# Two key pages turned within the query list, and two more loaded behind them

## The chip, the cores and the metric

The kernel runs on one core of a Trainium2 chip. The metric is the device time in microseconds (us) of one execution. TensorE (PE) multiplies, VectorE (DVE), ScalarE (ACT) and GpSimd (POOL) do elementwise work, and SyncE (SP) does no arithmetic and issues most of the DMAs.

## What is computed

One inference step of a two-layer decoder trunk: layer 0 mixes tokens with a conformer convolution, layer 1 with stick-breaking attention, and a gated ConvFFN follows each. There are 512 tokens of a new prompt and 8 sequences of 4 new tokens each, which also attend to 256 cached tokens, held in 2 pages of 128 tokens per sequence. The part that matters here is the attention:

```python
qkv = (h @ attn_w_qkv[a]).reshape(b, t, 3, N_HEADS, HEAD_DIM)
k_past = jnp.take(cache_k[a], page_table, axis=0)...      # 8 sequences x 2 pages
z = einsum('bqhd,bkhd->bhqk', q, k_all) * HEAD_DIM**-0.5 + bias
log_fail = where(valid, log_sigmoid(-z), 0)
after = cumsum(log_fail, axis=3, reverse=True) - log_fail
weights = where(valid, exp(log_sigmoid(z) + after), 0)
out = einsum('bhqk,bkhd->bqhd', weights, v_all)
```

## The kernel before, in words

Activations lie in memory with the model dimension on the partitions: `xT` is 128 x 8 x 544, for 512 prompt and 32 new tokens. A float32 matrix product is made of three matmuls on a high and a low part: ACT casts the weights to a high part `whi` (L398), DVE subtracts it to get the low part `wlo` (L401), and PE runs whi·XH, whi·XL, wlo·XH. The raw weights come in 1 MB loads (`raw54` and so on) into two buffers. The load for a buffer is issued on SP at L361, within the function of the last `wlo` that reads the buffer, so it stands in SP's order where the planner put that subtraction.

A planner (`Plan`) sets the order of the work. Each operation is listed with an engine, a cost in us and what it reads and writes. `run` then plays the list with these costs and emits each engine's instructions in the order in which the play starts them. At run time the engines keep that order, and semaphores keep the dependencies. A page load is planned as 2 us on SP and 6 us to land. SP is taken as busy for 0.7 us with any operation.

Two of these lists meet here.

- The first one ends with `queries` (from L1775): the rest of the first ConvFFN, the norm, and the queries `qT`. The last four chunks of the queries use a Strassen-like product (`query_quad`), whose inputs are made with three temporaries of 544 columns in the unused end of `kT` (`inputs`, L1489 and L1537; ring `tt2`). ACT and DVE bring the products from PSUM into `qT` (L1883, L1886). The list ends on SP: `xT` is saved to DRAM, so that its memory can hold pages, and pages 0, 1 and 2 are loaded into `page_t[0..2]` (columns 0 to 3071 of `xT`) by `key_page` (L2041 to L2045). A page is 4 DMAs of 128 KB.
- The second one is the attention. `keys` and `values` project chunk after chunk (`project`, 24 matmuls for each half: 256 columns, then 288). Below, k0, k1, v0, k2 are the first projections, with the weights 148, 149, 150 and 151, and A and B are their halves. `keys` evacuates `kT` on ACT (L2201), transposes the new rows on DVE (`kr`, L2207) and stores them with 4 DMAs (L2212). `pair` makes units of attention between prompt tokens: logits `z` on PE (L2432), exp, ln and exp on ACT, a clamp (L2451), a scan (L2462) and a product (L2467) on DVE, then the transposition `t` on PE (L2474) and the products `av`.

The cached keys are used in `page_logits(m)`, for m from 0 to 3, four pages each. DVE transposes two pages into `kt`, which is the unused end of `kT`, and two into buffers of the ring `e` (all at L2283). Then PE makes 32 logit matmuls into `dz` (L2301): 16 from `kt`, then 16 from the `e` buffers. Page i goes into `page_t[i % 3]`, once DVE has transposed page i-3. All 16 key pages pass this way, and after them the 16 value pages, which POOL gathers (L2050).

PE is in order, as are all engines here: if an instruction waits, all behind it on that engine wait too.

Of the kernel before, what the change touches and what calls it, by code (L numbers as in the profile page):

```python
# [18 lines left out]
D = 1024  # L19
# [5 lines left out]
T = SEQ + NS  # L25
# [39 lines left out]
LATE_X = 0.6  # L65
LIFT = 10
PAGE_BUFS = 3
LATER = 1
WAITS = (2,5)
DUE = (3,1)  # L70
# [180 lines left out]
def tile_trunk(  # L251
# [9 lines left out]
    dve, act, pool, pe = nc.vector, nc.scalar, nc.gpsimd, nc.tensor  # L261
# [84 lines left out]
    class Ring:  # L346
# [28 lines left out]
        def prep(self, later=None, halves=False):  # L375
# [35 lines left out]
            else:  # L411
                later.insert(min(LATER, len(later)), low)

# [308 lines left out]
    plan = Plan(E_CONV, 0.12, CONV_SHIFTS)  # L722
# [14 lines left out]
    def psum(tag):  # L737
        def make():
            if tag == "acc":
                taken.append(tag)  # L740
            return bank(tag, uid(tag))

        return plan.tile(tag, banks[tag], make)
# [363 lines left out]
    for c in range(0, NC, 2):  # L1107
# [9 lines left out]
        for cc in range(2):  # L1117
            plan.op("act", 0.33, lambda c=c, cc=cc, pt=pt: act.copy(
                ext_s[:, c + cc, :, 0:PAST], pt()[:, cc * 240:(cc + 1) * 240].rearrange("p (b t) -> p b t", b=NB)),
                r=[pt, "junk"], w=[("past", c + cc)])  # L1120
# [124 lines left out]
    for h, (c0, n) in enumerate(STREAMS):  # L1245
        if h:
            layer_norm(1)
        for g in (0, 4):
            for i in range(4):
                c = g + i  # L1250
# [5 lines left out]
        if not h:  # L1256
# [8 lines left out]
            r=[nrm.acc[0]], w=[ms])  # L1265
    plan.op("act", 0.34, lambda: act.activation(rs()[:, :n], ms()[:, :n], AF.Sqrt, bias=eps_t[:, 0:1], scale=1.0),
            r=[ms, "table"], w=[rs])
    plan.op("dve", 1.7, lambda: dve.reciprocal(rs()[:, :n], rs()[:, :n]), w=[rs])
    for c in range(NC):
# [3 lines left out]
                r=[rs, ("x", c, 0)], w=[u])  # L1273
# [4 lines left out]
            r=[u, ("XH", c, 0)], w=[("XL", c, 0)], lift=NLIFT)  # L1278
# [26 lines left out]
    def ffn(l, before, after):  # L1305
# [10 lines left out]
        plan = Plan(E_FFN)  # L1316
# [459 lines left out]
        def queries(s):  # L1776
# [35 lines left out]
            for h, st in enumerate((SA, SB)):  # L1812
                c0, n = st
                for c in range(NC):
# [3 lines left out]
                            r=[pt], w=[("x", c, h)])  # L1818
# [32 lines left out]
            for i in range(ready, len(plan.ops)):  # L1851
                e, cost, f, deps = plan.ops[i]
# [45 lines left out]
            plan.op("dve", 0.6, decode_columns, r=["numbers"], w=["tables"])  # L1898
            plan.op("dve", 0.9, decode_masks, r=["tables"])
            for j in range(PAGE_BUFS):  # L1900
                plan.op("sp", 2.0, lambda j=j: key_page(page_t[j], j), r=["saved", "numbers"])
            return s

        first = slot_no[0]
# [21 lines left out]
        if l == 0:  # L1926
            s = queries(s)
# [10 lines left out]
        after = after()  # L1938
# [93 lines left out]
    att = {}  # L2032
    xsave = scratch.tile([P, NC * T], F32, name="xsave")
    xflat = xT.rearrange("p c t -> p (c t)")
    page_t = [xflat[:, i * D:(i + 1) * D] for i in range(PAGE_BUFS)]
    numbers = []
# [4 lines left out]
    def key_page(t, j):  # L2041

        pages = cache_k[0, bass.ds(numbers[j], 1)].rearrange("o (q p) (x h) d -> o x p q (h d)", p=32, x=4)
        for x in range(4):
            nc.sync.dma_start(out=t[32 * x:32 * x + 32, :].rearrange("p (q r) -> p q r", q=4), in_=pages[0, x])  # L2045
# [3 lines left out]
    def gather(t, j, src):  # L2049
        pool.indirect_dma_start(out=t, out_offset=None, in_=src,  # L2050
                                in_offset=bass.IndirectOffsetOnAxis(ap=idx[:, j:j + 1], axis=0))

    ffn(0, nrm, None)
    qT, kT, kT_s, dz = (att[k] for k in ("qT", "kT", "kT_s", "dz"))
# [19 lines left out]
    def place_q(bg):  # L2074
        for rows, x, q, src in placed(bg):
            dst = Qz[rows].rearrange("p (c q) (b r) -> p q c b r", q=4, b=4)[:, q, :, :, 4 * x:4 * x + 4]
            pool.tensor_copy(dst, src)
# [33 lines left out]
    plan = Plan()  # L2111
# [139 lines left out]
    def page(i):  # L2251

        t = plan.tile("page", PAGE_BUFS, lambda: page_t[i % PAGE_BUFS])
        if i < PAGE_BUFS:
            plan.op("held", 0.0, lambda: None, w=[t])
            return t
        if i < 2 * NB:
            plan.op("sp", 2.0, lambda: key_page(t(), i), w=[t, ("asked", i)])
        else:
            plan.op("pool", 1.05, lambda: gather(t(), i % (2 * NB), cv), w=[t, ("asked", i)])  # L2260
        plan.op(f"page{i}", 6.0 if i < 2 * NB else 4.0, lambda: None, r=[("asked", i)], w=[(t, 1)])
        return t
# [7 lines left out]
    def page_logits(m):  # L2270

        bg = m // 2
        if m % 2 == 0:
            zt[bg] = psum("dz")
            if bg:
                plan.op("pool", 4.5, lambda: place_q(1), w=["Qz"])
        z = zt[bg]
        for odd in range(2):
            for pg in range(2):
                t = page(4 * m + 2 * odd + pg)  # L2280

                def turn(t=t, pg=pg, odd=odd):
                    dve.transpose(second[pg]() if odd else kt[:, pg * D:(pg + 1) * D], t())  # L2283

                plan.op("dve", 1.25, turn, r=[t, (t, 1), "pages"], w=[("ktq" if odd else "ktp", pg)],
                        a=[second[pg]] if odd else [])

        def logits():
            for odd in range(2):
                b = 2 * (m % 2) + odd  # L2290
                c0 = 32 * b - 16 * odd
                if odd:
                    parts = [(pg * P, P, second[pg]()) for pg in range(2)]
                else:
                    parts = [(0, KW, kt)]
                for e in range(2):
                    for lo, n, src in parts:
                        keys_of = src.rearrange("p (q k j) -> p k q j", k=NC, j=32)
                        for u in range(4):
                            k = 4 * (u % 2) + 2 * (u // 2) + e  # L2300
                            pe.matmul(z()[32 * u:32 * u + 32, (m % 2) * KW + lo:(m % 2) * KW + lo + n],  # L2301
                                      Qz[:, k, c0:c0 + 32], keys_of[:, k],
                                      start=(b == e == 0), stop=(b == 3 and e == 1), skip_group_check=True)

        plan.op("pe", 1.72, logits, r=[(k, i) for k in ("ktp", "ktq") for i in range(2)] + ["Qz", *second], w=[z], form="c32")
        if m % 2:
            for g in range(2):
                plan.op("dve", 0.45, lambda g=g: dve.tensor_scalar(
                    Zd[:, 2 * bg + g, :], z()[:, g * KW:(g + 1) * KW], bcol[:, 0:1], None, op0=ALU.add),
                    r=[z], w=[f"Zd{bg}", ("Zd", 2 * bg + g)])  # L2310
# [47 lines left out]
    def sequence(n):  # L2358

        t, b = n // 2, n % 2  # L2360
        ts = [page(2 * NB + 2 * n + pg) for pg in range(2)]
        pt = psum("dz")

        def f():
            for pg in range(2):
                values_of = ts[pg]().rearrange("p (x h d) -> p h x d", x=4, h=4)
                for u in range(4):
                    pe.matmul(pt()[32 * u:32 * u + 32, :2 * P], wT[:, t, pg, 32 * u:32 * u + 32], values_of[:, 2 * (u % 2) + u // 2],
                              start=(pg == 0), stop=(pg == 1), skip_group_check=True)

        plan.op("pe", 0.9, f, r=[*ts, *((x, 1) for x in ts), ("wT", t), "pages"], w=[pt], form="c32")

        o, m = oacc[:, t, :], own[:, b:b + 1]
        if b == 0:
            plan.op("act", 0.35, lambda: act.mul(o, pt()[:, :2 * P], m), r=[pt], w=[("oacc", t), ("Zd", t), f"Zd{t // 2}"])
        else:
            plan.op("dve", 0.37, lambda: dve.scalar_tensor_tensor(o, pt()[:, :2 * P], m, o, op0=ALU.mult, op1=ALU.add),
                    r=[pt], w=[("oacc", t)])
# [148 lines left out]
    for c in range(NC):  # L2527
        if c < 2:
            for m in range(2 * c, 2 * c + 2):
                page_logits(m)  # L2530
        if c == 2:
            decode_weights()
        if c + 2 < NC:
            both_halves(keys, c + 2)
        if c == 5:
            new_rows(kT_s, [("kT_s", i) for i in range(NC)], ksv)
            new_logits()
        if c + 1 < NC:
            both_halves(values, c + 1)
        if c == 5:  # L2540
            new_weights()
        if c == 7:
            new_rows(vT_s, [("vT_s", i) for i in range(NC)], vsv)
        for n in {3: (0,), 4: (1, 2), 5: (3, 4), 6: (5, 6), 7: (7,)}.get(c, ()):
            sequence(n)
        if c == 7:
            for bg in range(2):
                new_values(bg)
        if c == 7:
            while held_out:  # L2550
                held_out.pop(0)()
        pair(c)
# [5 lines left out]
    for i, tag in enumerate(("acc", "z", "z", "one")):  # L2558
# [3 lines left out]
        for q in range(4):  # L2562
            last = plan.op("pe", 6 * SA[1] * COL, weighted(pt, o0 + i, 0, q), w=[pt], follows=last,
                           r=[("slot", o0 + i)] + [("X", k) for k in (2 * q, 2 * q + 1)])
# [59 lines left out]
```

## Time and profile before

| What | Value |
|---|---|
| median of 3 runs | 1257.95 us (1257.33 to 1258.29) |
| the profiled execution | 1256.83 us, of which the span of its instructions is 1255.1 us |
| PE busy | 1239.3 us (99%) |
| DVE, ACT, POOL busy | 1011.2, 709.8, 173.8 us |
| mean granted clock of TensorE | 0.998 of full speed |
| moved by DMA | 142.40 MB |

Times in a profile are us from the start of the span. The query list ends about 631 us, where PE starts k0; the attention list ends about 832 us. In a timeline row the columns are start, duration, engine, line, operation, tiles, shapes and count; a bracket holds the idle time of the engine before it and what ended that. SPq is SP's own queue of issues: its duration is that of the issue, not of the transfer.

### The profile page before, as it was taken

The numbers are of one execution on the slowest core, as the hardware profiler recorded it, in microseconds if no ns is written. First come the engines' busy times: TensorE is split into PE (matmuls) and PEld (weight loads), VectorE is DVE, ScalarE is ACT, GpSimd is POOL, SyncE is SP. The second block draws the span as 40 slices with busy tenths as digits, with TensorE's granted clock in tenths as the row PEclk, the third lists the DMA queues.
The fourth block names the chain that finished last, engine by engine and source line by source line (L and its number), as shares of the span: only waits on it lengthen the run. The fifth ranks groups of instructions, "written<-read, shape, count | busy, mean of one in ns | idle before, by whom it ended". The sixth has DMA issues, their size and how long they took to land.

```text
span 1255.1 us, 26652 instructions
## 1 busy us (share of the span) xinstructions
PE 1239.3 (99%) x10742; PEld 1187.2 (95%) x10742; DVE 1011.2 (81%) x1700; ACT 709.8 (57%) x1421; POOL 173.8 (14%) x363
## 2 busy tenths in 40 slices
PE   9999999999999999999999999999999999999997
PEld 8997699999999999999988888999999999999997
DVE  7999887988987886878969897646979987887863
ACT  7793584646655454445545887744636645455453
POOL 5000014111001000000242344000101001000000
PEclk9999999999999999999999999999999999999999
DMA  7455423123233233244379465232123232233121
GB/s 223 129 168 152 129 68 117 35 86 114 80 112 118 68 106 99 92 145 161 97 190 246 128 173 159 71 126 85 49 88 102 93 120 93 80 108 118 60 79 72
DMA packets 139661, 142.40 MB, mean 113 GB/s; under 512 B 24045, under 2 KB 132773, under 8 KB 139266
## 3 DMA queue, kind: packets, MB, share of 16 engines
q1 hardware_dynamic: 133134, 120.29, 32.1%
q0 software_dynamic: 6400, 20.41, 5.2%
q8 instruction: 84, 1.38, 0.5%
q14 instruction: 39, 0.32, 0.1%
q10 hardware_dynamic: 4, 0.01, 0.0%
HBM read 129.34 MB, written 12.18 MB: 113 GB/s over the span
## 4 chain that ended last, share of the span: by engine, by line
PE 81%; DVE 14%; DMA 2%; ACT 2%; issue 1%; SPq 0%; POOL 0%; DVEq 0%; ACTq 0%
PE acc L1635 5%; PE acc L1634 5%; PE acc L1633 5%; PE acc L759 4%; PE acc L760 4%; PE acc L761 4%; PE av L896 3%; DVE wlo L401 3%; PE av L1412 3%; PE av L1413 3%; PE av L1414 3%; PE tr L1413 3%; PE tr L1412 3%; PE tr L1414 3%; PE tr L1633 3%; PE tr L1635 3%
## 5 line engine op out<-in xcount | busy, mean ns | idle before, releaser
L398 ACT CAST whi<-raw 128x1024 fp32r<-128x1024 f32 (+2 forms) x247 | 224.7, 913 | 123.5 <-PE av L1413 24.8
L401 DVE TENSOR_TENSOR wlo<-raw,whi 128x1024 fp32r<-128x1024 f32 (+2 forms) x247 | 258.7, 1050 | 33.0 <-ACT whi L398 31.5
L759 PE MATMUL acc<-XH,whi 128*128 128x288 f32 (+1 forms) x384 | 112.7, 294 | 0.0
L761 PE MATMUL acc<-XH,wlo 128*128 128x288 f32 (+1 forms) x384 | 110.3, 287 | 0.9 <-DVE wlo L401 0.9
L760 PE MATMUL acc<-XL,whi 128*128 128x288 f32 (+1 forms) x384 | 110.3, 287 | 0.0
L1412 PE MATMUL av<-HH,whi 128*128 128x288 f32 (+1 forms) x280 | 83.2, 297 | 0.5 <-DVE xT L1735 0.5
L1413 PE MATMUL av<-HL,whi 128*128 128x288 f32 (+1 forms) x280 | 82.6, 295 | 0.0
L1635 PE MATMUL acc<-TH,wlo 128*128 128x272 f32 x288 | 82.6, 287 | 0.0
L1634 PE MATMUL acc<-TL,whi 128*128 128x272 f32 x288 | 82.6, 287 | 0.0
L1633 PE MATMUL acc<-TH,whi 128*128 128x272 f32 x288 | 82.5, 287 | 0.0
L1414 PE MATMUL av<-HH,wlo 128*128 128x288 f32 (+1 forms) x280 | 82.2, 293 | 0.0
L1682 ACT COPY G<-acc 128x272 f32<-128x272 f32 (+1 forms) x72 | 26.8, 372 | 93.8 <-PE acc L1635 93.8
L2163 PE MATMUL acc<-XH,whi 128*128 128x256 f32 (+1 forms) x264 | 79.7, 302 | 0.0
L1412 PE MATMUL tr<-HH,whi 128*128 128x256 f32 (+1 forms) x280 | 78.5, 280 | 0.0
L1413 PE MATMUL tr<-HL,whi 128*128 128x256 f32 (+1 forms) x280 | 78.4, 280 | 0.0
L1414 PE MATMUL tr<-HH,wlo 128*128 128x256 f32 (+1 forms) x280 | 78.3, 280 | 0.0
L2165 PE MATMUL acc<-XH,wlo 128*128 128x256 f32 (+1 forms) x264 | 75.7, 287 | 0.0
L2164 PE MATMUL acc<-XL,whi 128*128 128x256 f32 (+1 forms) x264 | 75.7, 287 | 0.0
L759 PEld LDWEIGHTS acc<-XH,whi 128*128 128x128 f32 x384 | 72.2, 188 | 1.4 <-issue 0.4
L761 PEld LDWEIGHTS acc<-XH,wlo 128*128 128x128 f32 x384 | 72.1, 188 | 1.1 <-DVE wlo L401 1.1
L760 PEld LDWEIGHTS acc<-XL,whi 128*128 128x128 f32 x384 | 72.2, 188 | 0.3
L1573 DVE SCALAR_TENSOR_TENSOR cv<-G,fprm,cv 128x560 f32<-128x560 f32 x88 | 69.5, 797 | 0.5
(464 smaller groups left out, 4343.0 us busy)
## 6 DMA issues: line engine op xcount, KB each, us to landing
raw<-in_ffn_w_gate_dram SPq DMA_DIRECT2D x22, 1024.0 KB
raw<-in_ffn_w_up_dram SPq DMA_DIRECT2D x22, 1024.0 KB
raw<-in_ffn_w_down_dram SPq DMA_DIRECT2D x24, 768.0 KB
raw<-in_attn_w_qkv_dram SPq DMA_DIRECT2D x12, 1024.0 KB
xT<-in_cache_k_dram SPq DMA_DIRECT2D x64, 128.0 KB
raw<-in_conv_w_in_dram POOLq DMA_DIRECT2D x6, 1024.0 KB, 6.8
rep<-glu SPq DMA_DIRECT2D x36, 142.0 KB
raw<-in_conv_w_out_dram POOLq DMA_DIRECT2D x4, 1024.0 KB, 6.4
```

What stands on the lines that cost most here:

```text
L398: act.copy(hi[:, k, :], src[:, k])
L401: dve.tensor_tensor(lo[:, k, :], src[:, k], hi[:, k, :], op=ALU.subtract)
L759: pe.matmul(o, hi[:, k, :], XH[:, k, c0:c0 + n], start=(k == 0), stop=False)
L760: pe.matmul(o, hi[:, k, :], XL[:, k, c0:c0 + n], start=False, stop=False)
L761: pe.matmul(o, lo[:, k, :], XH[:, k, c0:c0 + n], start=False, stop=(k == NC - 1))
L1412: pe.matmul(o, hi[:, j + k, :], xh, start=(start and k == 0), stop=False, **kw)
L1413: pe.matmul(o, hi[:, j + k, :], xl, start=False, stop=False, **kw)
L1414: pe.matmul(o, lo[:, j + k, :], xh, start=False, stop=(stop and k == len(xs) - 1), **kw)
L1633: pe.matmul(o, hi[:, j + k, :], xh, start=(start and k == 0), stop=False, **kw)
L1634: pe.matmul(o, hi[:, j + k, :], xl, start=False, stop=False, **kw)
L1635: pe.matmul(o, lo[:, j + k, :], xh, start=False, stop=(k == 3), **kw)
L2163: pe.matmul(o, hi[:, k, :], XH[:, k, c0:c0 + n], start=(k == 0), stop=False)
```

## The change

Pages 0 and 1 are transposed into `kt` within the query list, once the last operation on the three temporaries (which lie in the same memory) is done. As soon as `page_t[0]` and `page_t[1]` are free of them, pages 3 and 4 are loaded there, in the query list too. In the attention list, `page` issues no load for pages 0 to 4, and `page_logits(0)` has no transposition for pages 0 and 1.

```diff
+EARLY_PAGES = 2
...
             for j in range(PAGE_BUFS):
-                plan.op("sp", 2.0, lambda j=j: key_page(page_t[j], j), r=["saved", "numbers"])
+                plan.op("sp", 2.0, lambda j=j: key_page(page_t[j], j), r=["saved", "numbers"], w=[("asked", j)])
+                plan.op(f"page{j}", 6.0, lambda: None, r=[("asked", j)], w=[("page", j)])
+            temps = [op for b in plan.rings["tt2"] for op in b.users]
+            for j in range(EARLY_PAGES):
+                def early(j=j):
+                    even = att["kT"].rearrange("p c t -> p (c t)")[:, 4 * T + j * D:4 * T + (j + 1) * D]
+                    dve.transpose(even, page_t[j])
+
+                plan.op("dve", 1.25, early, w=[("page", j)], after=temps)
+                plan.op("sp", 2.0, lambda j=j: key_page(page_t[j], PAGE_BUFS + j), w=[("page", j)])
             return s
...
-        if i < PAGE_BUFS:
+        if i < PAGE_BUFS + EARLY_PAGES:
             plan.op("held", 0.0, lambda: None, w=[t])
             return t
...
                 t = page(4 * m + 2 * odd + pg)
+
+                if 4 * m + 2 * odd + pg < EARLY_PAGES:
+                    plan.op("held", 0.0, lambda: None, r=["pages"], w=[("ktp", pg)])
+                    continue
```

The planner plays the changed list anew, so the order moves on all engines from here to the middle of the attention. On SP the 8 DMAs of pages 3 and 4 stand between the loads raw55 and raw56; before, they stood behind raw57. The order of the following DMAs is now raw56, raw57, page 5, a store of `kr`, page 6, a store of `kr`, raw58, page 7, page 8, a store of `kr`, page 9.

The first place is on DVE, at the end of the query list. `wlo147` is the last low part for the queries, `wlo148` the first one for k0, and the rows of `qT` take products out of PSUM. Before:

```order
L401 TENSOR_TENSOR wlo147_8091<-raw53_7541,whi147_8090 128x512
L1886 SCALAR_TENSOR_TENSOR qT_7678<-tr_457_8097,qT_7678 128x272
L1886 SCALAR_TENSOR_TENSOR qT_7678<-acc_454_8008,qT_7678 128x272
L401 TENSOR_TENSOR wlo148_8138<-raw54_7990,whi148_8137 128x1024
L401 TENSOR_TENSOR wlo149_8141<-raw54_7990,whi149_8140 128x1024
```

And after the change, at the same place on DVE:

```order
L402 TENSOR_TENSOR wlo147_8091<-raw53_7541,whi147_8090 128x512
L1908 STREAM_TRANSPOSE kT_7679<-xT_72 128x1024
L1887 SCALAR_TENSOR_TENSOR qT_7678<-tr_457_8097,qT_7678 128x272
L1908 STREAM_TRANSPOSE kT_7679<-xT_72 128x1024
L1887 SCALAR_TENSOR_TENSOR qT_7678<-acc_454_8008,qT_7678 128x272
L402 TENSOR_TENSOR wlo148_8143<-raw54_7990,whi148_8142 128x1024
L402 TENSOR_TENSOR wlo149_8151<-raw54_7990,whi149_8150 128x1024
```

The two transpositions stand ahead of the two rows of `qT` and of the low parts for k0 and k1.

The second place is on PE, where the logits of pages 4 to 7 (m = 1) stand in the attention list. `z` and `t` belong to units of prompt attention, `acc_486` and `whi151` to the second half of k2. Before:

```order
L2165 MATMUL acc_486_8622<-XH_73,wlo151_8192 128x288
L2432 MATMUL z_489_8658<-kT_7679,qT_7678 128x512
L2432 MATMUL z_490_8660<-kT_7679,qT_7678 128x512
L2301 MATMUL dz_471_8477<-kT_7679,xT_72 32x256 x8
L2301 MATMUL dz_471_8477<-e_460_8338,xT_72 32x128 x4
L2301 MATMUL dz_471_8477<-e_467_8421,xT_72 32x128 x4
```

After the change, in the middle of the second half of v0 (`e_460` and `e_461` hold pages 6 and 7):

```order
L2446 MATMUL z_480_8557<-kT_7679,qT_7678 128x256
L2446 MATMUL z_481_8559<-kT_7679,qT_7678 128x256
L2315 MATMUL dz_465_8393<-kT_7679,xT_72 32x256 x8
L2315 MATMUL dz_465_8393<-e_460_8307,xT_72 32x128 x4
L2315 MATMUL dz_465_8393<-e_461_8316,xT_72 32x128 x4
```

These logits have moved up from the end of k2 into the second half of v0, so 54 projection matmuls fewer stand ahead of them. The logits of pages 0 to 3 have moved up too, from the end of the first half of v0 to three quarters of the first half of k1, 54 projection matmuls earlier.

## Prediction

> **What bounds the kernel now.** I read the page, PE's waits in the attention, the stretches by 4 us, and then the timelines of DVE, SP, ACT and PE from 620 to 672 us. The page says what pays:
>
> ```profile
> span 1255.1 us, 26652 instructions
> ...
> PE 1239.3 (99%) x10742; PEld 1187.2 (95%) x10742; DVE 1011.2 (81%) x1700; ACT 709.8 (57%) x1421; POOL 173.8 (14%) x363
> ```
>
> PE is the bound. The change alters no matmul, only their order, so it can win what PE waits for and no more. PE's waits from 625 to 840 us (total, times, longest):
>
> ```profile
> PE t L2474 <- DVE e L2467: 1.4, 1, 1.4
> PE one L2193 <- ACT vT_s L2223: 1.4, 1, 1.4
> PE t L2474 <- ACT e L2477: 0.7, 1, 0.7
> PE one L2193 <- ACT vT L2221: 0.4, 1, 0.4
> PE acc L497 <- DVE xT L2577: 0.3, 1, 0.3
> ```
>
> The first two, 2.8 us, lie at 654 and 661 us, near the moved steps; the others come after 770 us. So 2.8 us are to be won there, if no new wait appears. Behind both is a late DVE:
>
> ```profile
> 623.22 0.44 DVE L1886 SCALAR_TENSOR_TENSOR qT<-tr,qT 128x272 f32<-128x272 f32 x1 [0.67 <-PE tr L1635]
> 624.70 0.44 DVE L1886 SCALAR_TENSOR_TENSOR qT<-acc,qT 128x272 f32<-128x272 f32 x1 [1.04 <-PE acc L1635]
> 625.06 2.35 DVE L401 TENSOR_TENSOR wlo<-raw,whi 128x1024 fp32r<-128x1024 f32 x2
> ...
> 633.59 2.36 DVE L401 TENSOR_TENSOR wlo<-raw,whi 128x1024 fp32r<-128x1024 f32 x2 [1.30 <-ACT whi L398]
> 635.87 2.37 DVE L2283 STREAM_TRANSPOSE kT<-xT 128x1024 f32<-128x1024 f32 x2
> ...
> 644.03 1.25 DVE L2283 STREAM_TRANSPOSE e<-xT 128x1024 f32<-128x1024 f32 x1 [2.91 <-DMA xT<-in_cache_k_dram]
> ...
> 651.98 0.45 DVE L2207 STREAM_TRANSPOSE kr<-kT 128x256 f32<-128x256 f32 x1 [2.89 <-DMA out_dram<-kr]
> ```
>
> DVE waits 2.9 us for page 3 and 2.9 us for a store, while the DMA engines were free just before (columns: PE, PEld, DVE, ACT, POOL busy, granted clock, DMA share, GB/s):
>
> ```profile
> 632.00:636.00 4.00, 4.00 (x34) 4.00 (x33) 2.70 (x4) 3.46 (x4) 3.37 (x7) 1.00 0.00 0
> 648.00:652.00 4.00, 4.00 (x55) 3.26 (x44) 1.11 (x2) 0.00 (x0) 0.00 (x0) 1.00 1.00 262
> ```
>
> **Part by part: the start.** Two transpositions leave 635.87 (2.37 us). At the new place they have 0.67 + 1.04 = 1.7 us of idle DVE, so the low parts behind them end 0.7 us late, 628.1 instead of 627.4. PE needs them from 631 us: free. SP's issues are not:
>
> ```profile
> 627.43 0.37 SPq L361 DMA_DIRECT2D raw<-in_attn_w_qkv_dram  x1
> 635.98 0.37 SPq L361 DMA_DIRECT2D raw<-in_attn_w_qkv_dram  x1
> 637.14 4.73 SPq L2045 DMA_DIRECT2D xT<-in_cache_k_dram  x8
> 647.84 4.95 SPq L2045 DMA_DIRECT2D xT<-in_cache_k_dram  x8
> 592.04 6.29 SPq L2045 DMA_DIRECT2D xT<-in_cache_k_dram  x12
> ```
>
> These are raw56, raw57, then pages. Pages 3 and 4 now stand ahead of raw56. The first transposition ends about 623.8, eight issues take 4.7 us, so raw56 goes out at 628.5, 1.1 us late. Who waits for raw56 is ACT, with all that is queued behind it:
>
> ```profile
> 632.51 2.01 ACT L398 CAST whi<-raw 128x1024 fp32r<-128x1024 f32 x2 [0.69 <-DMA raw<-in_attn_w_qkv_dram]
> 634.53 1.28 ACT L484 ACT_TABLE_LOAD   x1
> 635.83 0.38 ACT L2201 COPY kT<-acc 128x256 f32<-128x256 f32 x1
> ```
>
> That copy frees the accumulator bank with which PE starts k1 at 636.75; 1.1 us later it ends at 637.3, so PE waits 0.5 us. On DVE the two low parts end at 637.1 instead of 635.95, and pages 2 and 3 are turned by 639.4. PE reaches its first logits, after 18 matmuls of 0.12 us, at 639.4: at most 0.1 us more. Page 3, issued about 624, is there by then. This term is 0.6 us, and it may grow. The 1 MB of pages lies ahead of raw56 in the queue, and no row shows what that does to its landing: between nothing and another 1.5 us (1 MB at the 262 GB/s above is 4 us, of which the part after 628.5 counts). I take nothing, since raw55 is nearly through by 628. By the Trainium skill, "DMA: Bandwidth & Descriptors", section "Queues, rings and completion order", each DMA engine takes descriptors in the order of its ring, so the pages' bytes go first; by it the upper end would hold, and the forecast would rise by 1 us.
>
> **The second logits.** PE needs pages 6 and 7 for them. How fast pages come is set by SP and by the time to land:
>
> ```profile
> 640.11 5.27 DMA xT<-in_cache_k_dram
> 647.20 4.65 DMA out_dram<-kr
> ```
>
> In a busy queue an issue takes 4.95/8 = 0.62 us, in a quiet one 6.29/12 = 0.52. Page 5 can start when page 2 is turned, at 638.3. From there to the end of page 7 stand 21 issues (three pages, two stores, raw58): the last starts at 638.3 + 20 x 0.62 = 650.7 and lands, 4.65 to 5.27 us later, at 655.4 to 656.0. DVE needs these durations (busy, mean ns):
>
> ```profile
> L2283 DVE STREAM_TRANSPOSE e<-xT 128x1024 f32<-128x1024 f32 x8 | 9.8, 1230 | 5.2 <-DMA xT<-in_cache_k_dram 5.2
> L401 DVE TENSOR_TENSOR wlo<-raw,whi 128x1024 fp32r<-128x1024 f32 x7 | 8.4, 1206 | 2.5 <-ACT whi L398 2.5
> L2467 DVE TENSOR_TENSOR e<-e,s 128x1024 f32<-128x1024 f32 x4 | 5.1, 1268 | 0.0
> L2462 DVE TENSOR_TENSOR_SCAN s<-ones,s 128x512 f32<-128x512 f32 x4 | 4.9, 1215 | 0.0
> L2451 DVE TENSOR_SCALAR e<-e 128x1024 f32<-128x1024 f32 x5 | 3.3, 665 | 0.0
> L2225 DVE COPY vtok<-one 128x256 f32<-128x256 f32 x6 | 2.4, 402 | 0.2 <-PE one L2193 0.2
> L2462 DVE TENSOR_TENSOR_SCAN s<-ones,s 128x384 f32<-128x384 f32 x2 | 1.8, 917 | 0.0
> L2308 DVE TENSOR_SCALAR Zd<-dz,bcol 128x256 f32<-128x256 f32 x4 | 1.7, 460 | 0.0
> L2462 DVE TENSOR_TENSOR_SCAN s<-ones,s 128x128 f32<-128x128 f32 x2 | 0.7, 394 | 0.0
> ```
>
> Page 6, the 12th issue, lands about 650.1 and is turned by 651.3; two scans, a low part and a clamp follow (1.2 + 1.2 + 1.2 + 0.7), to 655.6. So page 7 is turned about 656.9, by either road. When is PE there?
>
> ```profile
> 654.04 0.28 PE L2165 MATMUL acc<-XH,wlo 128*128 128x256 f32 x1
> ...
> 668.94 1.14 PE L2432 MATMUL z<-kT,qT 64*128 64x384 f32 x8
> 670.00 0.38 PE L2163 MATMUL acc<-XH,whi 128*128 128x256 f32 x1
> ```
>
> (The shape shown for a merged row is that of its first instruction.) At 654.16, after its 150th projection matmul, PE before has done all that the changed order puts ahead of its second logits, 18 projection matmuls too many (2.3 us) and four small z too few (half of the 1.14). So PE would be there at 652.4, at 653.0 with the 0.6, and runs the first 0.6 us of the logits, which need only pages 4 and 5. It then waits from 653.6 to 656.9: 3.3 us where it waited 1.4. The cover that is gone is the 54 projection matmuls that stood ahead of these logits.
>
> **The transposition of the second unit.** Next PE needs the second product of a unit (`e_475`), behind this on DVE: copy, product, two scans, page 8 (0.4 + 1.27 + 1.83 + 1.23, to 661.6); page 9, the 33rd issue, lands at 638.3 + 32 x 0.62 + 4.65 to 5.27 = 662.8 to 663.4 and is turned by 664.3; then two Zd, a low part, a copy, page 10, two scans, two clamps and the product, 7.1 us. As timeline rows overlap by 0.08 us, I take off 0.7: 670.7, or 669.2 if page 9 does not wait. I take 670.2. At that point the changed PE has 12 projection matmuls fewer behind it (186 against 198) than PE before at 670.00, and all else alike: it is where PE before was at 670.0 - 1.5 = 668.5. So the lag is 1.7 us, between 0.7 and 2.6 (page 9 at once, or 0.4 us later still).
>
> **The sum.** New waits of 0.6, 3.3 and about 1, less the 2.8 that go, and less some time in which PE changes between kinds of matmuls under these waits: the lag of 1.7 us counts all of this. After it DVE has as much behind it as before at that time, PE has projection matmuls left to fill gaps, and the orders join again before the last pairs, so I carry 1.7 to the end. Profiled: 1256.83 + 1.7 = 1258.5. That execution is 1.1 us under the median of the runs, 1257.95, against which I give **1259.6 us**. About 2.5 us (0.2%) is what can be told from no change; the forecast lies within.
>
> **Rivals.**
>
> Faster: the DMA engines, relieved of 1 MB, go at the quiet pace (0.52 an issue, 4.65 to land), and pages come before PE. Then page 7 lands at 638.3 + 10.4 + 4.65 = 653.4, page 6 at 648.7, DVE's own chain ends at 655.4, and PE still waits near 2 us. To win the full 2.8 us (1255.1), pages would have to come 3 us earlier still. For it: DVE's 5.8 us of waits on DMA, gone. Against it: the share of 1.00 at 648 us, with as many DMAs as before.
>
> Slower: the second logits' wait costs PE its clock. No wait here is over 1.4 us, and the granted clock stays 1.00, but at the span's end, where PE is often idle, it falls:
>
> ```profile
> 1200.00:1255.00 55.00, 47.31 (x384) 46.54 (x383) 25.35 (x52) 23.49 (x48) 3.04 (x4) 0.95 0.21 71
> ```
>
> If a wait of 3.3 us at 653.6 halves the clock, the 4 us of matmuls behind it (rest of the logits, a transposition, half of v0) take 4 us more; 1 us of it hides under the next wait: a lag of 4.7, 1262.7 us. It decides from a wait a little longer than the 3.3 forecast. By the Trainium skill, "TensorE: Matmul & The Clock Gate", section "Why this matters for your kernels", idle gaps over about 3 us between bursts drop the clock to half; no run here shows such a gap, and by this rule this rival would be as likely as not.
>
> Nothing: 64 DMAs of key pages still pass one queue, and filling the idle DVE at 623 us only moves its waits. Every lag is then made up before 700 us: 1258.0. For it: DVE's list is no shorter by then. Against it: PE is in order and at 99%, so a lag is not made up.
>
> **Chances.** Forecast 0.45, faster 0.13, slower by the clock (or by raw56 landing 1.5 us later) 0.27, nothing 0.15. Range: 1256.0 to 1263.5, from half of the win to the slower rival. Faster by over 0.2%: 0.11; slower: the rival's 0.27 and a tenth from the upper part of the forecast, 0.37; within: 0.52.
>
> **What would show it.** In the profile after: raw56 issued near 628.5; page 7 turned near 657; a wait of PE for an `e` turned at L2297 of about 3.3 us; no wait for `vT_s` at 654; a wait of `t` for DVE near 669; the clock at 1.00 throughout. The forecast is wrong if pages 6 and 7 are turned before PE comes (then faster), or if the clock falls behind that wait (then slower).

## The result, and the profile after

| What | Before | After |
|---|---|---|
| median of 6 runs each | 1258.05 us (1256.46 to 1258.37) | 1265.83 us (1265.13 to 1267.7) |
| the profiled execution | 1256.83 us, span 1255.1 | 1267.6 us, span 1265.7 |
| mean granted clock | 0.998 | 0.995 |

The ratio is 1.0068, with a 95% interval of 1.0057 to 1.0079. The change costs 7.8 us, and the time lies above the range that was given. The profiled execution of the changed kernel is 1.8 us above the median of its runs and that of before 1.2 us under it, so the difference of the two profiles is larger than that of the medians. The page of the changed kernel shows the same work, 5 us more of it in PE's busy time, and 10.6 us more of span:

```profile
span 1265.7 us, 26656 instructions
...
PE 1244.3 (98%) x10742; PEld 1190.8 (94%) x10742; DVE 1010.2 (80%) x1700; ACT 708.7 (56%) x1421; POOL 174.5 (14%) x363
```

1.3 us of the 10.6 arise ahead of the change: raw55 is issued at 622.58 us in the kernel before and at 623.87 in the changed one. The row of before:

```profile
622.58 0.40 SPq L361 DMA_DIRECT2D raw<-in_attn_w_qkv_dram  x1
```

So 1.3 us are to be taken off times of the changed profile before they are held against times of before, and 9.3 us are left to explain. SP's issues in the changed kernel, with raw55, the eight DMAs of pages 3 and 4, then raw56 and raw57 merged in one row:

```profile
623.87 0.40 SPq L362 DMA_DIRECT2D raw<-in_attn_w_qkv_dram  x1
625.02 4.59 SPq L2055 DMA_DIRECT2D xT<-in_cache_k_dram  x8
629.99 12.28 SPq L362 DMA_DIRECT2D raw<-in_attn_w_qkv_dram  x2
```

raw56 goes out at 629.99 (628.7 on the scale of before), as forecast. ACT stands for it, with all that is queued behind this cast:

```profile
638.37 1.99 ACT L399 CAST whi<-raw 128x1024 fp32r<-128x1024 f32 x2 [4.94 <-DMA raw<-in_attn_w_qkv_dram]
640.38 1.28 ACT L485 ACT_TABLE_LOAD   x1
641.68 0.65 ACT L2211 COPY kT<-acc 128x256 f32<-128x256 f32 x2
```

The cast starts 8.4 us after the issue (638.37 - 629.99); in the kernel before it was 5.1 (632.51 - 627.43). The table load and the copy of `kT` follow in a row, and the copy frees PE's bank. PE's waits, from 600 to 860 us (total, times, longest):

```profile
PE acc L2173 <- ACT kT L2211: 3.6, 1, 3.6
PE one L2203 <- ACT vT L2231: 2.0, 1, 2.0
PE t L2488 <- ACT e L2491: 1.5, 2, 0.8
PE dz L2315 <- DVE e L2297: 1.2, 1, 1.2
PE t L2488 <- DVE e L2481: 0.6, 1, 0.6
PE t L2488 <- ACT vT L2231: 0.5, 1, 0.5
PE av L1634 <- ACT qT L1884: 0.4, 1, 0.4
```

They sum to 9.8 us, against 4.2 in the kernel before. And behind the two longest ones the clock falls, in stretches of 2 us (the columns are those of the prediction's table; the third figure from the right is the granted clock):

```profile
640.00:642.00 2.00, 0.00 (x0) 0.00 (x0) 2.00 (x3) 1.97 (x4) 1.92 (x3) 0.99 0.00 0
642.00:644.00 2.00, 1.90 (x9) 1.90 (x10) 2.00 (x2) 1.35 (x4) 1.67 (x9) 0.50 0.39 101
644.00:646.00 2.00, 2.00 (x15) 1.87 (x18) 1.93 (x4) 0.00 (x0) 1.83 (x5) 0.66 1.09 385
...
706.00:708.00 2.00, 1.17 (x6) 1.17 (x7) 2.00 (x6) 1.81 (x4) 1.15 (x1) 0.71 0.00 0
708.00:710.00 2.00, 2.00 (x10) 1.78 (x9) 2.00 (x5) 1.97 (x2) 0.00 (x0) 0.50 0.03 8
710.00:712.00 2.00, 2.00 (x16) 1.61 (x16) 2.00 (x4) 0.77 (x3) 0.00 (x0) 0.94 0.45 130
```

Each fall takes 2 x (0.01 + 0.50 + 0.34) = 1.7 us, or 2 x (0.29 + 0.50 + 0.06) = 1.7 us, from PE: 3.4 us at half speed. So the account of PE closes: 5.6 us more of waits and 3.4 us of lost clock make 9.0 of the 9.3 us.

The second logits, where the prediction put its largest wait, wait 1.2 us only. The rows of PE there, and of DVE for page 7:

```profile
660.74 0.40 PE L2315 MATMUL dz<-e,xT 128*32 128x128 f32 x8
662.32 0.86 PE L2315 MATMUL dz<-e,xT 128*32 128x128 f32 x24 [1.18 <-DVE e L2297]
```

```profile
661.02 1.25 DVE L2297 STREAM_TRANSPOSE e<-xT 128x1024 f32<-128x1024 f32 x1 [1.92 <-DMA xT<-in_cache_k_dram]
```

Page 7 is turned at 662.3 (661.0 on the scale of before, forecast 656.9), but PE, held up before, comes late too.

### The profile page after: what moved, and what is told of

Same layout as the page of the kernel before. It is cut to its first block, busy times and chain, and to the rows that moved or that the text cites. A ratio compares the mean times of both kernels' runs of the same rounds, so it can differ in the third digit from the quotient of the medians.

```text
span 1265.7 us, 26656 instructions
## 1 busy us (share of the span) xinstructions
PE 1244.3 (98%) x10742; PEld 1190.8 (94%) x10742; DVE 1010.2 (80%) x1700; ACT 708.7 (56%) x1421; POOL 174.5 (14%) x363
## 4 chain that ended last, share of the span: by engine, by line
PE 78%; DVE 14%; ACT 2%; DMA 2%; issue 2%; SPq 1%; POOL 0%; DVEq 0%; POOLq 0%; ACTq 0%
PE acc L1636 5%; PE acc L1635 5%; PE acc L1634 5%; PE acc L760 4%; PE acc L761 4%; PE acc L762 4%; PE av L897 3%; DVE wlo L402 3%; PE av L1413 3%; PE av L1414 3%; PE av L1415 3%; PE tr L1414 3%; PE tr L1413 3%; PE tr L1415 3%; PE tr L1634 2%; PE tr L1636 2%
```

## The experiments

Theory A: the cost is the 1 MB of pages ahead of raw56. It lands late, ACT and the bank behind it are late, and PE's long wait takes the clock down. Theory B, its rival: the cost is the new order of the attention list, in which logits and transpositions stand ahead of their data. Times are medians, beside runs of the kernel before on the same chip (1257.3 to 1257.5 us in these). What is said of waits and of the clock is read from one profiled execution of each kernel, and from 600 to 860 us. The diffs show the lines that decide; lines that only carry a value along are left out.

### Pages behind raw56

`issues[max(issues)]` is the low part whose function issues raw56, and `True` keeps each DMA behind what SP has been given so far.

```diff
-                plan.op("sp", 2.0, lambda j=j: key_page(page_t[j], PAGE_BUFS + j), w=[("page", j)])
+                plan.op("sp", 2.0, lambda j=j: key_page(page_t[j], PAGE_BUFS + j, True), w=[("page", j)], after=[issues[max(issues)]])
```

> The changed kernel, but the 8 page DMAs of the query list (pages 3 and 4) stand on SP behind raw56 and not ahead of it. The order of PE, DVE and ACT is that of the changed kernel, row for row. Theory A (the 1 MB of pages ahead of raw56 delays its landing, ACT with the accumulator bank behind it, and PE's long wait takes the clock down): raw56 goes out about 1 us earlier than in the changed kernel and lands within 5 to 6 us of its issue (there 8.3); PE's wait for the first kT copy falls from 3.6 us to under 1; the granted clock stays at 1.00 behind it; the time falls from 1265.8 us by 5 to 8 us, to 1258 to 1261. Theory B (the new order of the attention list costs the time, above all logits that stand 54 matmuls too early): the first wait may go, but the waits behind it stay, and the time is 1263 us or more.

1262.92 us, ratio 1.0043 (1.0029 to 1.0056). raw56 is cast 5.7 us after its issue, the first wait is gone, and another one is there:

```profile
PE dz L2321 <- DVE e L2303: 3.0, 1, 3.0
PE one L2209 <- ACT vT L2237: 2.4, 1, 2.4
PE t L2494 <- ACT e L2497: 1.6, 2, 0.9
PE t L2494 <- ACT vT L2237: 0.5, 1, 0.5
PE acc L2179 <- ACT kT L2217: 0.5, 1, 0.5
```

The second logits now wait 3.0 us for page 7, and the clock falls there:

```profile
656.00:658.00 2.00, 0.00 (x0) 0.00 (x0) 0.54 (x1) 1.88 (x5) 0.46 (x2) 1.00 1.13 220
658.00:660.00 2.00, 1.24 (x24) 0.97 (x24) 2.00 (x3) 0.00 (x0) 0.88 (x2) 0.58 1.01 206
660.00:662.00 2.00, 2.00 (x17) 1.80 (x10) 2.00 (x4) 0.59 (x1) 1.73 (x4) 0.57 1.03 226
```

Theory A named the first wait rightly, but its sum was 2 us short: moving the pages behind raw56 wins 2.9 us. The late PE had covered a wait that the new order has anyway.

### The load alone, in the order of before

```diff
             self.raw[self.nraw] = t
+            if self.nraw == 55:
+                for j in range(2):
+                    key_page(page_t[j], j, True)
             self.nraw += 1
```

> The kernel before, and 8 page DMAs more: between raw55 and raw56 pages 0 and 1 are loaded a second time into their own places, so 1 MB of the same kind stands ahead of raw56. No transposition is moved, and the order of PE, DVE and ACT is that of the kernel before, row for row. Theory A: raw56 goes out 1 to 3 us later and lands 7 to 9 us after its issue (before 5.0), PE waits 2 to 5 us for the first kT copy, the granted clock falls below 0.9 in the 8 us behind that, and the time is 4 to 8 us above the kernel before (1262 to 1266). Theory B: a transfer that stands in the queue changes no order, and the time is within 1 us of the kernel before (1258).

1261.95 us, ratio 1.0036 (1.0023 to 1.0048): 4.7 us more, just under what Theory A expected, with no transposition moved. ACT casts raw56 8.3 us after its issue at 629.78, and PE waits:

```profile
638.12 1.99 ACT L403 CAST whi<-raw 128x1024 fp32r<-128x1024 f32 x2 [4.89 <-DMA raw<-in_attn_w_qkv_dram]
```

```profile
PE acc L2170 <- ACT kT L2208: 3.5, 1, 3.5
```

The clock falls by 1.7 us behind it. So 1 MB in this place of the queue costs PE a wait and a fall of the clock by itself. Theory B's "within 1 us" is refuted; neither theory is the whole.

### The transpositions alone

Pages 3 and 4 are loaded by the attention list again:

```diff
-                plan.op("sp", 2.0, lambda j=j: key_page(page_t[j], PAGE_BUFS + j), w=[("page", j)])
...
-        if i < PAGE_BUFS + EARLY_PAGES:
+        if i < PAGE_BUFS:
```

> The changed kernel with the two early transpositions, but pages 3 and 4 are loaded from the attention list as in the kernel before, so no page stands ahead of raw56 in the list (two single DMAs of 128 KB come ahead of it all the same). The order of the attention list is its own, since its planner now sees pages 3 and 4 come later. Theory A: raw56 lands 5 to 6 us after its issue, PE's wait for the first kT copy is under 1.5 us, the time is 1257 to 1261 us. Theory B (moving the transpositions themselves costs, or the logits come too early): 1262 us or more, with waits of PE for transposed pages of over 2 us.

1260.32 us, ratio 1.0026 (1.0016 to 1.0036). There is no wait for the bank, raw56 is cast 5.7 us after its issue; but PE waits 2.3 us for a product of DVE and 2.2 us for `vT`, and the clock falls once. The time is in Theory A's range; the waits are as long as Theory B's, but not for transposed pages. The planner had made a third order here, so this run could not part them.

### PE kept busy in its first wait

```diff
+        if c == 1 and not h:
+            spare = psum("t")
+            def idle():
+                for _ in range(26):
+                    pe.matmul(spare()[:, :256], W.w[k0][0][:, 0, :], XH[:, 0, :256], start=True, stop=True)
+            order[0] = plan.op("pe", 0.0, idle, w=[spare], after=[order[0]])
         pt = project(k0 + TURNS.index(("k", c)), h)
```

> The changed kernel with 26 matmuls of 128 x 256 more on PE, ahead of k1, where it waits 3.6 us for the kT copy; their result, in an unused PSUM bank, is not read. All other orders are those of the changed kernel. They take 26 x 0.117 = 3.0 us of the wait. If the fall of the clock behind the wait (0.75 and 0.83 over 8 us in the changed kernel, 1.7 us of matmul time) is part of the cost and comes from PE standing idle: the clock stays at 1.00 from 640 to 648 us and the time falls by 1 to 3 us, to 1263 to 1265. If the cost is all waiting, or the clock falls for another reason: 1265.8 us within 0.7, or up to 0.5 above it, with the clock below 0.9 in the same place.

1268.06 us, ratio 1.0086 (1.0073 to 1.01): not faster, and above both ranges that were expected; that it is slower than the changed kernel is not shown, as the intervals overlap. The clock does stay at 1.00 from 636 to 656 us, and PE's first logits come 1.8 us earlier than in the changed kernel (642.8 against 644.6, on the scale of before). But the second logits then wait 2.4 us instead of 1.2, and the fall of the clock comes there:

```profile
PE dz L2323 <- DVE e L2305: 2.4, 1, 2.4
```

So it is PE's standing idle that takes the clock down: with PE busy in this place, the fall is gone from it. What the filler saves here is lost in the next place, where PE waits for pages.

### PE kept busy in its second wait

As the first experiment, with 22 such matmuls on the weights of v0, behind the second quarter of its second half:

```diff
             plan.fill.add(last)
+            if (slot - k0, h, q) == (2, 1, 1):
+                spare = psum("t")
+                def idle():
+                    for _ in range(22):
+                        pe.matmul(spare()[:, :256], W.w[slot][0][:, 0, :], XH[:, 0, :256], start=True, stop=True)
+                last = plan.op("pe", 0.0, idle, w=[spare], after=[last])
         order[0] = last
```

> As e1_raw_first (the pages behind raw56), and 22 matmuls of 128 x 256 more on PE just ahead of the second logits, where e1_raw_first waits 3.0 us for page 7 and its clock then falls to 0.79 and 0.96 (1.6 us of matmul time); their result is not read. They take 22 x 0.117 = 2.6 us of that wait. If PE's standing idle is what takes the clock down, and its loss there is carried to the end: clock 1.00 from 656 to 680 us and 1261 to 1262 us, 1 to 2 under e1_raw_first. If the next waits take back what the clock gave (in e6_fill they did): 1262.9 us within 0.8, or up to 2 above it, with the clock at 1.00 there and other waits longer.

1261.53 us, ratio 1.0033 (1.0021 to 1.0045). There is no fall of the clock in the whole list (in the profiled execution, 1263.72 us, the longest of the six). The median is 1.4 us under the first experiment, near the 1.7 of one fall, but the two intervals overlap, so a gain is not shown.

### The order of before kept

The first experiment, but the planner is left to believe in the old work; nothing is emitted for it:

```diff
-        if i < PAGE_BUFS + EARLY_PAGES:
+        if i < PAGE_BUFS:
...
-            plan.op("sp", 2.0, lambda: key_page(t(), i), w=[t, ("asked", i)])
+            plan.op("sp", 2.0, lambda: None if i < PAGE_BUFS + EARLY_PAGES else key_page(t(), i), w=[t, ("asked", i)])
...
-                if 4 * m + 2 * odd + pg < EARLY_PAGES:
-                    plan.op("held", 0.0, lambda: None, r=["pages"], w=[("ktp", pg)])
-                    continue
                 def turn(t=t, pg=pg, odd=odd):
+                    if 4 * m + 2 * odd + pg < EARLY_PAGES:
+                        return
```

> As e1_raw_first, but the planner of the attention list is left to believe that pages 0 and 1 are still turned there and pages 3 and 4 still loaded there (both at their old cost, with nothing emitted). So PE and ACT have the order of the kernel before row for row, DVE has it but for the two transpositions, which stand in the query list, and only SP's order differs by the 8 page DMAs. Theory B2 (what e1_raw_first still loses comes from the new order of the attention list, in which logits stand ahead of their pages): the waits of 3.0 and 2.4 us go, the waits are those of the kernel before or less, the clock stays at 1.00, and the time is 1255 to 1258.5 us. Theory C (moving two transpositions and two pages costs by itself, by the low parts that come 0.7 us late or by pages that meet raw57): 1260 us or more in the old order too.

1254.24 us, ratio 0.9975 (0.9964 to 0.9985): 3.2 us faster than the kernel before, a little more than was expected, and the best version of this study. All that PE waits for from 600 to 860 us:

```profile
PE t L2492 <- ACT e L2495: 0.7, 1, 0.7
PE one L2209 <- ACT vT L2237: 0.2, 1, 0.2
```

0.9 us instead of 4.2, and the clock stays at 1.00. Moving two transpositions and two pages is a gain, by the 2.8 us of waits at 654 and 661 us that the prediction had named as all that could be won. Theory C is refuted.

### The fourth corner

Two orders and two places of the pages make four kernels, the corners of a table; this one was missing. It is the order of before kept, with the pages ahead of raw56 as in the changed kernel:

```diff
-                plan.op("sp", 2.0, lambda j=j: key_page(page_t[j], PAGE_BUFS + j, True), w=[("page", j)], after=[issues[max(issues)]])
+                plan.op("sp", 2.0, lambda j=j: key_page(page_t[j], PAGE_BUFS + j), w=[("page", j)])
```

> As e8_old_order (order of PE, DVE and ACT as there), but the 8 page DMAs stand ahead of raw56, as in the changed kernel. It is the fourth corner: with the new order, moving the pages behind raw56 was worth 2.9 us (1265.8 to 1262.9); with the order of before, the load alone cost 4.7 us (e3_loads_only). If the late landing of raw56 is a cost of its own, and there are few waits left behind it that could take it up (0.9 us in e8_old_order): PE waits about 3.5 us for the first kT copy, the clock falls below 0.9 behind that, and the time is 4 to 6 us over e8_old_order, 1258 to 1260.5. If it only counts where the order is tight: within 2 us of e8_old_order, under 1256.5.

1260.38 us, ratio 1.0024 (1.0014 to 1.0033). As expected, PE waits 3.5 us, and the clock falls, here to half for 6.8 us, twice as long as in the other runs:

```profile
PE acc L2173 <- ACT kT L2211: 3.5, 1, 3.5
```

```profile
638.00:640.00 2.00, 0.00 (x0) 0.00 (x0) 1.94 (x2) 1.98 (x3) 1.92 (x3) 0.78 0.00 0
640.00:642.00 2.00, 1.29 (x6) 1.29 (x7) 2.00 (x4) 1.96 (x5) 1.72 (x7) 0.50 0.17 40
642.00:644.00 2.00, 2.00 (x11) 2.00 (x11) 2.00 (x3) 0.00 (x0) 1.82 (x5) 0.50 1.01 339
644.00:646.00 2.00, 2.00 (x11) 1.91 (x9) 0.50 (x1) 0.00 (x0) 1.67 (x9) 0.51 1.13 268
```

The four corners, as differences of medians to the kernel before:

| | order of before | new order |
|---|---|---|
| raw56 first | -3.2 us | +5.6 us |
| pages first | +2.9 us | +7.8 us |

The new order costs 8.8 us where raw56 comes first, 4.9 where the pages do. The pages ahead of raw56 cost 6.1 us in the old order and 2.2 in the new one. The two costs cover each other in part: a PE that is late at k1 has less to wait at the second logits.

### Half the load

As the load alone, with one page of 4 DMAs (0.5 MB):

```diff
-                for j in range(2):
-                    key_page(page_t[j], j, True)
+                key_page(page_t[0], 0, True)
```

> As e3_loads_only, with 4 page DMAs (0.5 MB) between raw55 and raw56 instead of 8. There 1 MB made raw56 land 8 us after its issue, PE wait 3.5 us and the clock fall to 0.72 and 0.85, at a cost of 4.7 us. If the bytes ahead set the landing, raw56 is issued at about its old time and lands 6 to 7 us after that, PE waits 1 to 2 us, and, as no wait under 2 us has taken the clock down here, the clock stays at 1.00: 1258.4 to 1259.6 us, less than half of the cost of the 1 MB. If the clock falls for any wait and the cost goes by halves: 1259.8 us with a clock under 0.95 from 640 to 648 us. If raw56 is not late with 0.5 MB: 1257.4 us within 0.6.

1258.55 us, ratio 1.0007 (0.9998 to 1.0016): not to be told from the kernel before. raw56 is cast 5.9 us after its issue, less late than expected, and no wait for `kT` is left. (The four issues end 2.2 us ahead of raw56's own, the eight of the 1 MB 0.4 us ahead, so the bytes are not the only difference.) The delay shows later, and I had not expected a fall of the clock there:

```profile
PE one L2199 <- ACT vT_s L2229: 2.4, 1, 2.4
```

This is the wait of 1.4 us of the kernel before, 1 us longer, and the clock loses 1.7 us behind it. This is the profiled execution, the longest of the 11; in six of them the mean clock is 0.998, as in the profile of before, which has no fall in the list.

### A third buffer for `kr`

```diff
-        kr = sbuf("kr", 2 * P, 2)
+        turn = len(plan.rings.get("kr", [])) % 3
+        kr = plan.tile("kr", 2, lambda: new_s if turn == 2 else va.tile([P, 2 * P], F32, tag=f"kr{turn}", name=uid("kr"), bufs=1))
```

> As e1_raw_first, but the tile kr (new keys on their way to the cache) has three buffers in turn where it had two, the third in memory that xT leaves unused; the order of all engines is unchanged. If the wait of 2.4 us near 704 us (PE for vT from ACT) comes down the chain from DVE, which stands 3.0 us at 694 us for a store of kr that is queued behind a 1 MB raw load: DVE's wait goes, PE's falls under 1 us, and the time is 1260 to 1261.7 us. If DVE's wait is covered: 1262.9 us within 0.8.

> The kernel before with three buffers for kr where it had two; all orders unchanged. There DVE stands 2.9 us at 649 us for a store of kr, and behind it PE waits 1.4 us at 654 and 1.4 at 661 us. If that store is what makes these waits: they fall by 1.5 to 2.8 us together and the time to 1254.5 to 1256. If page 6 and the scans behind it come no earlier without that wait: 1257.3 us within 0.7.

On the first experiment: 1261.53 us, ratio 1.003 (1.0019 to 1.0042), 1.4 us less with overlapping intervals. PE's wait of 2.4 us becomes two, 1.3 us in all. What the third buffer took away is DVE's wait in the row of the first experiment:

```profile
696.64 0.45 DVE L2223 STREAM_TRANSPOSE kr<-kT 128x256 f32<-128x256 f32 x1 [2.99 <-DMA out_dram<-kr]
```

On the kernel before: 1256.69 us, ratio 0.9997 (0.9988 to 1.0006), no difference. DVE's wait for the store falls from 2.9 to 0.3 us, but DVE then stands 3.9 us for a page, so PE's two waits stay, at 1.3 and 1.1 us.

### An order in between

The first experiment, with this part of the order kept: the planner believes in the two transpositions, not in the two loads.

```diff
-                if 4 * m + 2 * odd + pg < EARLY_PAGES:
-                    plan.op("held", 0.0, lambda: None, r=["pages"], w=[("ktp", pg)])
-                    continue
                 def turn(t=t, pg=pg, odd=odd):
+                    if 4 * m + 2 * odd + pg < EARLY_PAGES:
+                        return
```

> As e1_raw_first, but the planner of the attention list is left to believe that the two transpositions are still made there (2.5 us of VectorE at its start), while it knows that pages 3 and 4 are in place. Its order lies between the two: the second logits stand behind 156 projection matmuls from k0 on (132 in e1_raw_first, 186 in e8_old_order and before), the third behind 228 (210, 270). If logits that stand too early are the cost, it lies between too: 24 matmuls (2.9 us) later, the second logits wait under 1 us and keep the clock, but what stands behind them is still too early by 30 to 40 matmuls: 1257 to 1261 us. If another difference of the orders makes the cost: at either end, 1254.2 or 1262.9 us within 1.

1262.07 us, ratio 1.0038 (1.0025 to 1.005). The second logits no longer wait, and the clock does not fall, but PE waits 6.1 us in seven places. (The profiled execution, 1260.34 us, is the fastest of the six; in the two slowest of the others the mean clock is lower, 0.996 and 0.995 against 0.998.) The order with the second logits 24 matmuls later is not shown to be better than that of the first experiment, so the cost does not follow from how many matmuls too early they stand. With raw56 ahead of the pages, every order that the planner made anew (the changed kernel's, this one, and that of the transpositions alone, where two page DMAs stay ahead) lies 3.0 to 5.6 us over the kernel before; only the old one keeps the gain.

## Why the prediction was wrong

Two steps failed: that raw56's landing adds nothing ("I take nothing"), and that the lag of 1.7 us is carried to the end. At the transposition of the second unit, where the forecast had PE 1.7 us behind, the changed kernel is 4.5 us behind (674.25 us, 673.0 on the scale of before, against 668.5), and 9.3 at the end. In the first experiment, with raw56 on time, it is 1.9 us there, about as forecast though partly for another reason (one fall of the clock is in it), and 5.8 at the end.

**raw56.** The issue was right (1.1 us late forecast, 1.3 measured), and so was the chain of ACT, table load, copy and bank. The step that failed is its landing: "no row shows what that does to its landing: between nothing and another 1.5 us ... I take nothing". It was another 3.3 us (8.4 against 5.1), shown by the load alone (8.3). PE's wait was 3.6 us where 0.5 was forecast. The reason given, that raw55 is nearly through by 628, counted the wrong bytes: what lay ahead were the pages themselves. The prediction's own rates would have said so, if the pages' bytes are taken to follow raw55's: ACT's cast of raw55 starts at 627.76 in the kernel before, and 4 us of pages behind that end 3.3 us after 628.5 (an estimate from the rows of before). With half the pages, sent off earlier, it was 0.8 us (5.9). By the Trainium skill, "DMA: Bandwidth & Descriptors", section "Queues, rings and completion order", the pages' bytes go first. The traces agree with that (8.4 us with the pages ahead, 5.1 without); the upper end that I had drawn from it, 1.5 us, was too low.

**The second logits.** The wait of 3.3 us and page 7 at 656.9 us are what the first experiment shows once raw56 is on time: 3.0 us, and page 7 turned at 657.8 on the scale of before. In the changed kernel the first error hid it: PE was late, page 7 came 4 us later too, and the wait was 1.2 us.

**The clock.** The forecast let it stay at 1.00 and gave its fall to a rival, "from a wait a little longer than the 3.3 forecast". It fell behind a wait of 2.0 us already, and the changed kernel has two falls. The rival's size was off as well: 1.7 us for one fall, not 4 less 1. Its sum, 1262.7 us, is near the first experiment's 1262.9 by chance, since other waits make up the rest. By the Trainium skill, "TensorE: Matmul & The Clock Gate", section "Why this matters for your kernels", gaps over about 3 us do it; the traces differ, with a fall behind 2.0 us.

**The second unit.** A wait of `t` of about 1 us near 669 us does not exist, neither in the changed kernel nor in the first experiment: PE came later than the product. In the first experiment the product is there at 669.7 us on the scale of before (forecast 670.2) and PE at 670.4.

**To the end.** "I carry 1.7 to the end" failed too. Behind 700 us PE waits 2.0 + 1.5 + 0.5 = 4.0 us where the kernel before waits 0.7 + 0.4 + 0.3, and one fall of the clock lies there. In the first experiment it is 4.5 us of waits. Part of it comes from stores of `kr` behind a 1 MB load (the third buffer halved that wait); for the rest the four corners show that it belongs to the order, not which rows of it. In four runs (both fillers, the third buffer on the first experiment, the order in between) 1.2 to 2.2 us of the lag are neither waits nor clock nor filler; these stay open. That ACT's order (casts, table load, then the copy) could be turned round, so that the bank would not wait for raw56, was not tried.

**A reading.** The prediction says that the DMA engines were free just before both waits of DVE. That holds for page 3 (share 0.00 from 632 to 636 us), not for the store: the row from 648 to 652 us has a share of 1.00.

**What held.** That PE is the bound: for the changed kernel, the first experiment, the load alone and the order kept, waits and clock give +9.0, +5.5, +4.0 and -3.3 us against measured lags of +9.3, +5.8, +4.2 and -3.1 (for the fourth corner +3.8 against +2.9; 1.6 us of its fall, worth 0.8, lie in PE's wait). The four runs with an open rest are named above. And it held that 2.8 us were to be won.

## What to carry to other kernels

A transfer that is moved up in a queue is paid by what stands behind it there: ask which load is next, who waits for it, and how many bytes are still on their way when it is issued. When a planner makes a list anew, test the change with the old order held fixed as well; here the change was worth -3.2 us and the new order +8.8. Waits on one in-order engine are not a sum, since the first one covers the next, so a term can be right and still be missing from the total.

## What the runs showed of the hardware

- In these lists a fall of TensorE's clock always cost 1.7 us or twice that: 3.4 us at half speed, whatever the wait was. Waits of 3.6, 3.5, 3.0, 2.4, 2.3 and 2.0 us did it, while waits of 1.5 us and less never did. Length alone does not decide: one wait of 2.2 us, with the transpositions alone, and one of 2.4, at 702 us in the first experiment, left the clock at 1.00.

  What decides shows when the traces are cut at the changes of the clock. These lie on a grid with cells of 3.41 us: each fall of the changed kernel lasts one cell, that of the fourth corner two (6.83 us), and the two falls of the changed kernel begin at 641.97 and 706.82 us, which is 19 times 3.413 apart. The wait of 2.0 us ahead of the second fall lies within one cell, in which PE is busy for 1.47 us (the row below it is the fall):

```profile
703.41:706.82 3.41, 1.47 (x12) 1.26 (x11) 3.41 (x6) 3.38 (x8) 0.24 (x1) 1.00 0.01 2
706.82:710.24 3.42, 3.41 (x16) 3.19 (x18) 3.42 (x8) 2.99 (x4) 0.91 (x1) 0.50 0.02 5
```

  The wait of 2.4 us in the first experiment, from 701.92 to 704.29, is cut at 702.69 by the grid of its own run (counted from the fall at 658.32), and PE is busy for 2.64 and 1.82 us in the two cells:

```profile
699.28:702.69 3.41, 2.64 (x20) 2.36 (x18) 3.41 (x5) 2.68 (x4) 0.00 (x0) 1.00 0.06 10
702.69:706.11 3.42, 1.82 (x16) 1.70 (x16) 3.42 (x8) 3.20 (x7) 1.14 (x1) 1.00 0.03 7
```

  Over all 13 profiles, from 600 to 860 us, every cell ahead of a fall has 1.94 us or more of idle PE, and every other cell at full clock 1.61 or less. So what counts is the idle time within one cell, with a limit between 1.6 and 1.9 us. The grid lies differently in each run (a boundary stands 18.1 us behind raw55's issue in the changed kernel and 16.6 in the fourth corner, which is 1.0 and 3.0 us once whole cells are taken off), so a wait near the limit may cost a fall in one execution and not in the next; as each kernel has one profile, that is not shown. At the end of the span the clock falls behind cells with less idle time, down to 1.1 us; why is open.

  By the Trainium skill, "TensorE: Matmul & The Clock Gate", section "What's actually happening", activity is judged in free-running windows of 3.4 us. The length of each fall and the grid agree with that.

- A 1 MB load was ready for ACT 5.1 us after its issue with nothing behind it on SP for 8 us, 5.3 to 5.7 with pages issued right behind it, 5.9 with 0.5 MB ahead whose issues ended 2.2 us before its own, and 8.2 to 8.4 with 1 MB just ahead.
